# A decoder layer on one core: a residual whose bias row is added by a transfer, a shorter softmax, and another order of the first loads

## The chip, the cores and the metric

The kernel runs on one core of a Trainium2 chip. A core has a matrix engine (TensorE, PE in the profile, with its weight loads as PEld), a vector engine (VectorE, DVE), a scalar engine (ScalarE, ACT), a general engine (GpSimd, POOL) and SyncE (SP), and 16 DMA engines that move data between the large memory (HBM), the on-chip memory (SBUF) and within SBUF. Matrix products land in a separate small memory, PSUM, in banks of 512 floats a row. Every engine takes its instructions in order; they wait for one another by semaphores. The metric is the device time of one execution in microseconds (us), as the median of several.

## The reference

One decoder layer for 256 tokens of width 2048, all in float32:

1. `h = norm(alpha * x + 0.5 * swiglu(x))`, with a feed-forward block of inner width 5632. `norm` subtracts the mean of a token's row, divides by its standard deviation, multiplies by a gain row `g` and adds a bias row `b`.
2. A token mixer with two branches: attention with 16 heads (an indexer first picks 64 keys for every query, all others are masked; then a softmax over the scaled, masked scores and a weighted sum of the values), and a gated linear recurrence of width 2560. Both are gated, merged and multiplied by an output matrix: `h = norm(alpha * h + merged @ w_out)`.
3. `h = norm(alpha * h + 0.5 * swiglu(h))` with a second feed-forward block.

So there are three norms and three residual additions. Steps 2 and 3 need `alpha * h`, that is `alpha * (normalized * g + b)`, as the start of their sum.

## The kernel before, in words

**Products.** Every product is done in pairs of rounded numbers: a float32 weight piece `raw` is split into `wh` (rounded, ScalarE, line 243) and `wl` (the rest, VectorE, line 244), and activations likewise. Three matmuls, high by high, high by low, low by high, make one product (lines 694, 695, 697). In part of the products a scheme with seven in place of eight block products is used; for it VectorE makes sums of weight blocks (lines 206, 210, 213) and of activations (`left`, lines 592 to 598). The weights arrive as pieces of 128 x 1024 floats (`raw`, 512 KB) or of twice that (`rf`). Class `Weights` holds the list of all pieces in the order of use: `load_to` issues their transfers on SP, up to ten pieces ahead of use, into 5 `raw` buffers and 3 `rf` buffers; `split_to` issues the two splits, 4 pieces ahead, into 5 buffers; `unit` hands out the operands.

**Background steps.** Whenever `unit` takes up a new piece, it calls `bg.step()`, which advances every background generator by one `yield`. So a generator's `yield`s place its instructions in the program, one step per weight piece. The residuals, the heads' softmax and small tables are such generators.

**Order.** For PE, SP and POOL the order of the instructions is the order of the program text. For VectorE and ScalarE a planner sets the order from costs that it assumes; `issue_after(ins)` queues an instruction behind another one of the same engine. Whatever order comes out is then fixed: an engine whose next instruction has to wait holds up all that is behind it.

**Start.** Ten matmuls on a constant warm up PE (`warm_up`, line 439). The input `x`, transposed, is loaded in 8 chunks of 256 KB (`load_x_fm`, line 444), and each is split in two halves (`split_x`, lines 451 and 452). SP issues chunk 0, the first weight piece in two halves, chunk 1 and the second piece. The chunks 2 to 7 and the pieces 2 and 3 follow only when a one-column copy on VectorE (line 571), which writes into chunk 2's buffer, has waited for the first split. POOL issues the transfers of `cols` (224 columns of gains, biases and other per-channel values, line 459) and of `posi` (the positions, line 461) at once. `consts`, which makes sine and cosine tables from them, is a background generator.

**Residual.** `residual` prepares `alpha * (y * g + b)` in the tiles `Y[t][nb]`: two halves `t` of 128 tokens and four column blocks `nb` of 512. For each block POOL loads the rows of `g` and `b`, copied over all 128 partitions (`row`, line 649, 256 KB each), and in the first residual also two tiles of `Y` that had been put away in HBM (line 658). In the next steps VectorE does, for each `t`, `y = y * ALPHA * gr` (line 662) and `y = br * ALPHA + y` (line 664). With its `yield`s a block takes five steps. It runs twice: beside the merge of the two branches and the first part of the output product (1385 to 1466 us), and at the start of the second feed-forward block (1559 to 1622 us). The tiles `gr`, `br`, `Y` and many others share 53 buffers.

**Partial sums by transfer.** In the feed-forward blocks, halves of the output product are copied from PSUM with a factor (line 1109) and added to `Y` by a transfer of POOL with `accum_op=OP.add` (line 1110). These 80 transfers are the only adding ones.

**Heads.** `head` computes the scores of one head for two query blocks, 128 and 256 keys wide, into one PSUM tile of 384 columns. VectorE then scales them and adds the mask `bias`, which is 0 or -1e30 (line 1279), finds the negated maximum of each part (line 1284, two instructions), ScalarE takes the exponential with its sum (line 1287), VectorE divides (lines 1289, 1291), PE transposes (line 1295), ScalarE copies (line 1298) and PE multiplies by the values (lines 1301, 1302). Four heads are in work at a time, beside the products of the gates; at the end `bg.drain` runs what is left.

**End.** `OuterNorm.finish` normalizes the last tile of 128 tokens in four blocks. `first` (line 948) subtracts the mean and multiplies by `g`, `second` (line 952) multiplies by the inverse deviation and adds `b`, both on VectorE; for two of the blocks PE does the second part with a diagonal matrix (`by_pe`, line 967) and ScalarE copies the result (line 968). `leave` (line 956) issues the output transfers on SP.

Of the kernel before, what the change touches and what calls it, by code (L numbers as in the profile page):

```python
# [11 lines left out]
AF = mybir.ActivationFunctionType  # L12
OP = mybir.AluOpType
AX = mybir.AxisListType.X

P = 128
# [3 lines left out]
NK = D // P  # L20
# [9 lines left out]
ALPHA = 2.0 ** 0.25  # L30
THETA = 500000.0
TOPK = 64
NEG = -1e30
TAKEN = -3e38
ATT_SCALE = 128.0 ** -0.5
# [96 lines left out]
class Weights:  # L132
# [85 lines left out]
    def split_to(self, i, step=PIECE):  # L218
        nc = self.nc
        while self.split <= min(i, len(self.pieces) - 1):  # L220
            form = self.pieces[self.split][1]
            self.load_to(self.split)
            k = self.key(self.split)
            if self.split in self.wides:
                h, l = ([self.wide() for _ in range(2)] for _ in range(2))
                for c in range(2):
                    src = self.raw[k][:, c * 512:(c + 1) * 512]
                    nc.scalar.activation(h[c], src, AF.Copy)
                    nc.vector.tensor_tensor(l[c], src, h[c], op=OP.subtract)
                self.hl[self.split] = (h, l)  # L230
                del self.raw[k]
                self.split += 1
                continue
            h, l = (self.pool.tile([P, PIECE], F32R, name=f"w{s}{self.split}", tag=f"w{s}", bufs=HL_BUFS)
                    for s in "hl")
            n = self.size(self.split)
            if form:
                parts = [(self.operand(k, form), *(x[:, :n].rearrange("p (f r c) -> p f r c", r=4, c=P)
                                                   for x in (h, l)))]
            else:  # L240
                parts = [tuple(x[:, q:min(n, q + step)] for x in (self.raw[k], h, l)) for q in range(0, n, step)]
            for src, hp, lp in parts:
                nc.scalar.activation(hp, src, AF.Copy)  # L243
                self.last = nc.vector.tensor_tensor(lp, src, hp, op=OP.subtract)  # L244
            self.hl[self.split] = (h, l)
            if form in (None, FORMS[-1]):
                del self.raw[k]
            self.split += 1
# [71 lines left out]
def tile_layer(ctx, tc, x_fm, x_tm, pos, f1a, f1o, wA, wki, wB, wG, lru, wab, wrb, wo, f2a, f2o,  # L320
               cols_d, ln1_g, ln1_b, ln2_g, ln2_b, ln3_g, ln3_b, out):
    nc = tc.nc
# [4 lines left out]
    V, A, T, G = nc.vector, nc.scalar, nc.tensor, nc.gpsimd  # L327
# [96 lines left out]
    W = Weights(nc, pool, pieces, bg.step)  # L424
# [5 lines left out]
    xraw = [U("x") for _ in range(NK // 2)]  # L430
# [12 lines left out]
    def load_x_fm(k2):  # L443
        nc.sync.dma_start(xraw[k2], x_fm[:, k2 * 512:(k2 + 1) * 512])

    def split_x(k2):
        r = []
        for c in range(2):
            src = xraw[k2][:, c * S:(c + 1) * S]
            hl = UHL("xs")  # L450
            A.activation(hl[:, 0], src, AF.Copy)
            V.tensor_tensor(hl[:, 1], src, hl[:, 0], op=OP.subtract)
            r.append(hl)
        return r

    xs = []
    W.load_to(1, load_x_fm)
    cols = C([P, NCOLS], "cols")
    G.dma_start(cols, cols_d)
    posi = C([P, 2], "posi", I32)  # L460
    G.dma_start(posi, pos)
    tri = C([P, P], "tri")
    jp = tri.bitcast(I32)
    G.iota(jp, pattern=[[1, P]], base=0, channel_multiplier=-1)
# [21 lines left out]
        yield  # L486

    def consts():
        V.tensor_scalar(tri, jp, 0.0, NEG, op0=OP.is_gt, op1=OP.mult)
        posf = SM(2)  # L490
        V.tensor_copy(posf, posi)
        yield
        ang = SM(32)
        for t in range(2):
            V.tensor_scalar(ang[:, t * 16:t * 16 + 16], invf, posf[:, t:t + 1], None, op0=OP.mult)
        yield
        for dst, turn, shift in ((sn, 0.0, 0.0), (cs, 0.25, 1.5707963267948966)):
            k = SM(32)
            r = SM(32)
            V.tensor_scalar(k, ang, 0.15915494309189535, turn, op0=OP.mult, op1=OP.add)  # L500
            V.tensor_scalar(k, k, 12582912.0, None, op0=OP.add)
            V.tensor_scalar(k, k, 12582912.0, None, op0=OP.subtract)
            V.scalar_tensor_tensor(r, k, -6.28125, ang, op0=OP.mult, op1=OP.add)
            V.scalar_tensor_tensor(r, k, -0.0019350051879882812, r, op0=OP.mult, op1=OP.add)
            yield
            V.scalar_tensor_tensor(r, k, -3.019916050195849e-07, r, op0=OP.mult, op1=OP.add)
            V.tensor_scalar(r, r, shift, None, op0=OP.add)
            V.tensor_scalar(r, r, 3.1415925, -3.1415925, op0=OP.min, op1=OP.max)
            A.activation(dst.rearrange("p a b -> p (a b)"), r, AF.Sin)
            yield  # L510
# [56 lines left out]
    with tc.manual_schedule():  # L567
        for k2 in range(4):
            xs += split_x(k2)
            if k2 == 0:  # L570
                V.tensor_copy(xraw[2][:, :1], xs[0][:, 1, :1])
                W.load_to(3, load_x_fm)
                for j in range(4, NK // 2):
                    load_x_fm(j)
            W.split_to(k2, (256, 512, PIECE, PIECE)[k2])
        for k2 in range(4, NK // 2):
            xs += split_x(k2)

    def later(gen, ins):
        while True:  # L580
# [71 lines left out]
    def residual(g, b, away=None):  # L652
        for nb in range(4):
            gr, br = row(g, nb, "gr"), row(b, nb, "br")
            if away:
                for t in range(2):
                    Y[t][nb] = U("y")
                    G.dma_start(Y[t][nb], away[t][nb])
            yield
            for t in range(2):  # L660
                y = Y[t][nb]
                V.scalar_tensor_tensor(y, y, ALPHA, gr, op0=OP.mult, op1=OP.mult)
                yield
                V.scalar_tensor_tensor(y, br, ALPHA, y, op0=OP.mult, op1=OP.add)  # L664
                yield


# [249 lines left out]
    class OuterNorm(Norm):  # L917
# [18 lines left out]
        def finish(self):  # L936


            with tc.high_priority():
                self.chain(1)  # L940
            sums = {}
            for nb, o, w in ((0, 0, 512), (1, 0, S), (1, S, S)):
                ps = sums[nb, o] = BP()[:, :w]
                T.matmul(ps, ident, self.rows[1][nb][:, o:o + w], start=True, stop=False)

            def first(t, nb):
                y = Y[t][nb]
                V.scalar_tensor_tensor(y, y, self.mv[t], self.rows[0][nb], op0=OP.subtract, op1=OP.mult)

            def second(t, nb, o=0, w=512):  # L950
                y = Y[t][nb][:, o:o + w]
                V.scalar_tensor_tensor(y, y, self.r[t], self.rows[1][nb][:, o:o + w], op0=OP.mult, op1=OP.add)
                leave(t, nb, o, w)

            def leave(t, nb, o=0, w=512):
                nc.sync.dma_start(out[t * P:(t + 1) * P, nb * 512 + o:nb * 512 + o + w], Y[t][nb][:, o:o + w])

            for nb in range(4):
                first(0, nb)
            for nb in range(4):  # L960
                second(0, nb)
            diag = U("dg")[:, :P]
            A.activation(diag, ident, AF.Copy, scale=self.r[1])

            def by_pe(nb, o=0, w=512):
                ps, y = sums[nb, o], Y[1][nb][:, o:o + w]
                T.matmul(ps, diag, y, start=False, stop=True)
                A.activation(y, ps, AF.Copy)

            first(1, 2)  # L970
            first(1, 0)
            by_pe(0)
            second(1, 2)
            leave(1, 0)
            first(1, 1)
            by_pe(1, 0, S)
            by_pe(1, S, S)
            first(1, 3)
            second(1, 3, 0, S)
            second(1, 3, S, S)  # L980
            leave(1, 1)
# [159 lines left out]
    bias = C([P, 3 * P], "bias")  # L1141
# [126 lines left out]
    def head(h):  # L1268
# [5 lines left out]
        ps = BP()  # L1274
# [1 line left out]
        T.matmul(ps[:, P:3 * P], q[:, P:], k, start=True, stop=True)  # L1276
        yield
        s = U("s")[:, :3 * P]
        V.scalar_tensor_tensor(s, ps[:, :3 * P], ATT_SCALE, bias, op0=OP.mult, op1=OP.add)
        nm = SM(2)  # L1280
        sm = SM(2)
        part = (s[:, :P], s[:, P:])
        for t in range(2):
            V.tensor_reduce(nm[:, t:t + 1], part[t], axis=AX, op=OP.max, negate=True)
        yield
        for t in range(2):
            A.activation(part[t], part[t], AF.Exp, bias=nm[:, t:t + 1], accum_out=sm[:, t:t + 1])
        yield
        V.reciprocal(sm, sm)
        for t in range(2):  # L1290
# [2 lines left out]
        ps = BP()  # L1293
# [6 lines left out]
        ps = BP()  # L1300
# [61 lines left out]
    for nb in range(4):  # L1362
        g, got = got, fetch(ga[nb + 1]) if nb < 3 else None
        s, _ = product(ya, ya_forms, YA_FAST[nb])
# [71 lines left out]
    for j in range(NR + LAG):  # L1436
        if j < NR:
            s = block3(hs)
# [5 lines left out]
            for tap in (2, 1, 0):  # L1444
                sh = 3 - tap
                V.scalar_tensor_tensor(xc[:, sh:], raw[:, :S - sh], col("conv_w", tap * NR + j), xc[:, sh:],
                                       op0=OP.mult, op1=OP.add)
# [5 lines left out]
        if j >= LAG:  # L1453
# [6 lines left out]
            ps = banks[c - 1]  # L1460
            for n in range(2):
                mm3(ps[:, n * S:(n + 1) * S], xcs[i], W.unit(P), False, n == 1)
            vw, t = U("vw"), T1()
# [164 lines left out]
```

## Time and profile before

| | us |
|---|---|
| median of 3 runs | 2239.33 |
| lowest and highest | 2238.25, 2239.59 |
| the profiled execution, its own time | 2239.67 |
| its span in the profile | 2237.9 |
| PE busy in the span | 2223.3 |
| VectorE busy | 2106.7 |
| ScalarE busy | 1429.8 |
| POOL busy | 125.0 |

The profiled execution took 2239.67 us; 1.8 us of that lie outside its span. A row of a list of waits names an engine and a line, what it waited for, and the total, the number and the longest of these waits. A row of the timeline gives the start, the duration, the engine, the line, the operation, the tile written and the tiles read with their shapes, the number of instructions in the row, and in brackets the idle time ahead of it with what ended it. A row of a table by windows gives for each engine the busy time in that stretch and the number of its instructions, then the granted TensorE clock, the share of time in which the 16 DMA engines were busy, and GB/s. In a list by queue, q1 carries SP's transfers and q0 POOL's, with packets, megabytes and the share of the time of 16 engines. The ends of matmuls are modelled, so a gap of PE in these rows is somewhat shorter than the real one.

### The profile page before, as it was taken

What the parts mean: (1) busy time and instruction counts of PE and PEld (TensorE: products, weight loads), DVE (VectorE), ACT (ScalarE), POOL (GpSimd) and SP (SyncE); (2) the same over time, 40 slices, a digit from 0 to 9 for tenths busy, and PEclk for the clock granted to TensorE, in tenths of its full rate; (3) what the DMA queues carried; (4) which work ended last, traced back from release to release, by engine and by line L of the source; (5) the groups of instructions that cost most, each with busy time, mean ns of one, the idle gap of its engine ahead of it and who ended that gap; (6) DMA issues with size and microseconds to landing.
All of it is one profiled execution on the core that took longest, in us unless ns stands there. A gap on an engine that the chain in (4) does not pass through costs nothing. (4 is left out here: it accounts for less than half of the span.)

```text
span 2237.9 us, 38642 instructions
## 1 busy us (share of the span) xinstructions
PE 2223.3 (99%) x14582; PEld 2056.6 (92%) x14582; DVE 2106.7 (94%) x3037; ACT 1429.8 (64%) x1995; POOL 125.0 (6%) x195
## 2 busy tenths in 40 slices
PE   9999999999999999999999999999999999999998
PEld 7999999999998898899999999998889999999997
DVE  8999999999999999899868879999999999999997
ACT  7666666666656655665567786555666666666663
POOL 0000000000001000001000002100000000000001
PEclk9999999999999999999999999999999999999999
DMA  9776666666675555648666668766677667676655
GB/s 328 240 227 232 233 214 226 236 222 236 225 241 194 187 198 177 210 132 302 199 192 194 197 189 324 266 214 205 229 228 230 237 220 239 223 243 215 219 200 188
DMA packets 126186, 498.61 MB, mean 223 GB/s; under 512 B 14608, under 2 KB 17424, under 8 KB 107312
## 3 DMA queue, kind: packets, MB, share of 16 engines
q1 hardware_dynamic: 107424, 451.98, 57.9%
q0 software_dynamic: 18576, 44.17, 8.4%
q8 instruction: 114, 1.87, 0.3%
q14 instruction: 72, 0.59, 0.1%
HBM read 464.63 MB, written 10.49 MB: 212 GB/s over the span
## 5 line engine op out<-in xcount | busy, mean ns | idle before, releaser
L243 ACT ACTIVATE wh<-raw 128x1024 fp32r<-128x1024 f32 (+1 forms) x569 | 575.0, 1028 | 288.6 <-PE mm L695 164.4
L244 DVE TENSOR_TENSOR wl<-raw,wh 128x1024 fp32r<-128x1024 f32 (+1 forms) x569 | 661.9, 1183 | 79.8 <-ACT wh L243 78.6
L243 ACT ACTIVATE wh<-rf 128x1024 fp32r<-128x1024 f32 (+1 forms) x438 | 393.5, 915 | 191.6 <-PE mm L695 103.6
L244 DVE TENSOR_TENSOR wl<-rf,wh 128x1024 fp32r<-128x1024 f32 (+1 forms) x438 | 450.9, 1042 | 7.2 <-ACT wh L243 1.5
L694 PE MATMUL mm<-wh,hs 128*128 128x512 f32 (+1 forms) x872 | 297.3, 350 | 0.0
L695 PE MATMUL mm<-wh,hs 128*128 128x512 f32 (+1 forms) x872 | 292.1, 344 | 0.0
L694 PE MATMUL mm<-wh,g 128*128 128x512 f32 x656 | 249.5, 380 | 1.9 <-DVE z L1076 1.9
L695 PE MATMUL mm<-wh,g 128*128 128x512 f32 x656 | 248.8, 379 | 0.5 <-DVE g L810 0.5
L243 ACT ACTIVATE wh<-ws 128x1024 fp32r<-128x1024 f32 x146 | 155.2, 1063 | 123.9 <-PE mm L695 71.7
L694 PE MATMUL bp<-wh,sh 128*128 128x256 f32 x876 | 213.6, 278 | 0.0
L695 PE MATMUL bp<-wh,sl 128*128 128x256 f32 x876 | 210.7, 275 | 0.0
L697 PE MATMUL mm<-wl,hs 128*128 128x512 f32 (+1 forms) x872 | 205.0, 344 | 0.0
L206 DVE TENSOR_TENSOR ws<-rf 128x1024 f32<-128x1024 f32 x146 | 178.3, 1221 | 8.8 <-DMA rf<-wab 2.8
L244 DVE TENSOR_TENSOR wl<-ws,wh 128x1024 fp32r<-128x1024 f32 x146 | 178.1, 1220 | 2.8 <-ACT wh L243 2.6
L694 PEld LDWEIGHTS mm<-wh,hs 128*128 128x128 f32 x872 | 165.8, 190 | 15.3 <-issue 1.3
L695 PEld LDWEIGHTS mm<-wh,hs 128*128 128x128 f32 x872 | 165.9, 190 | 13.6
L1404 PE MATMUL mm<-hs,wh 128*128 128x256 f32 x640 | 176.4, 276 | 0.0
L1405 PE MATMUL mm<-hs,wh 128*128 128x256 f32 x640 | 176.0, 275 | 0.0
L1406 PE MATMUL mm<-hs,wl 128*128 128x256 f32 x640 | 176.0, 275 | 0.0
L695 PEld LDWEIGHTS bp<-wh,sl 128*128 128x128 f32 x876 | 168.1, 192 | 1.2
L694 PEld LDWEIGHTS bp<-wh,sh 128*128 128x128 f32 x876 | 168.0, 192 | 1.2
L697 PE MATMUL mm<-wl,g 128*128 128x512 f32 x656 | 168.3, 379 | 0.0
(374 smaller groups left out, 4886.5 us busy)
## 6 DMA issues: line engine op xcount, KB each, us to landing
rf<-f1a SPq DMA_DIRECT2D x57, 1024.0 KB, 6.2
rf<-f2a SPq DMA_DIRECT2D x57, 1024.0 KB, 6.0
raw<-f1o SPq DMA_DIRECT2D x88, 512.0 KB, 7.8
raw<-f2o SPq DMA_DIRECT2D x88, 512.0 KB, 7.8
raw<-wB SPq DMA_DIRECT2D x80, 512.0 KB, 4.5
raw<-f2a SPq DMA_DIRECT2D x62, 512.0 KB, 3.9
raw<-f1a SPq DMA_DIRECT2D x61, 512.0 KB, 3.9
raw<-wG SPq DMA_DIRECT2D x54, 512.0 KB, 4.2
```

Of the source, the lines that this page charges most:

```text
L206: v.tensor_tensor(t, b[:, 0:4:3], b[:, 1:2].to_broadcast([P, 2, 4, P]), op=OP.add)
L243: nc.scalar.activation(hp, src, AF.Copy)
L244: self.last = nc.vector.tensor_tensor(lp, src, hp, op=OP.subtract)
L694: T.matmul(ps, xh, w[0], start=start, stop=False)
L695: T.matmul(ps, xl, w[0], start=False, stop=False)
L697: T.matmul(ps, xh, w[1], start=False, stop=stop)
L1404: T.matmul(ps, w[0], xh, start=first, stop=False)
L1405: T.matmul(ps, w[0], xl, start=False, stop=False)
L1406: T.matmul(ps, w[1], xh, start=False, stop=last)
```

## The change

The change has five parts.

1. **First loads.** SP issues the chunks 0 to 3 of `x` and the pieces 0 to 3 in turn, and then chunks 4 to 7, with no wait. The one-column copy of line 571 goes.
2. **Column table.** `cols` and `posi` are no longer issued first. A one-column copy on VectorE writes into `cols` behind the last split of `x`, and POOL's two transfers wait for it. `consts` starts eight steps later.
3. **Residual.** ScalarE scales the bias row once a block (`br = ALPHA * br`, queued behind the newest `wh`), VectorE does only `y = y * ALPHA * gr`, and POOL adds `br` to `y` by a transfer, SBUF to SBUF, one for each `t`. Rows and the first product are two steps apart in place of one, and a block takes four steps in place of five. The adding transfers stand in POOL's queue ahead of the next block's rows.
4. **Heads.** One instruction a part reads the scores from PSUM, adds the mask, multiplies by `-ATT_SCALE` and finds the minimum; it replaces the scaling over both parts and the maximum of each. The exponential takes its input with a factor of -1.
5. **End.** `first(1, 0)` stands ahead of `first(1, 2)`.

```diff
@@ Weights.split_to
-                nc.scalar.activation(hp, src, AF.Copy)
+                self.last_h = nc.scalar.activation(hp, src, AF.Copy)
                 self.last = nc.vector.tensor_tensor(lp, src, hp, op=OP.subtract)
@@ tile_layer, start
-    W.load_to(1, load_x_fm)
+    W.load_to(3, load_x_fm)
+    for k2 in range(4, NK // 2):
+        load_x_fm(k2)
     cols = C([P, NCOLS], "cols")
-    G.dma_start(cols, cols_d)
     posi = C([P, 2], "posi", I32)
-    G.dma_start(posi, pos)
@@ consts
+        for _ in range(8):
+            yield
         V.tensor_scalar(tri, jp, 0.0, NEG, op0=OP.is_gt, op1=OP.mult)
@@ tile_layer, the first splits
             xs += split_x(k2)
-            if k2 == 0:
-                V.tensor_copy(xraw[2][:, :1], xs[0][:, 1, :1])
-                W.load_to(3, load_x_fm)
-                for j in range(4, NK // 2):
-                    load_x_fm(j)
             W.split_to(k2, (256, 512, PIECE, PIECE)[k2])
         for k2 in range(4, NK // 2):
             xs += split_x(k2)
+        V.tensor_copy(cols[:, :1], xs[-1][:, 1, :1])
+    G.dma_start(cols, cols_d)
+    G.dma_start(posi, pos)
@@ residual
             yield
+            yield
+            with tc.issue_after(W.last_h.ins):
+                A.activation(br, br, AF.Copy, scale=ALPHA)
             for t in range(2):
                 y = Y[t][nb]
                 V.scalar_tensor_tensor(y, y, ALPHA, gr, op0=OP.mult, op1=OP.mult)
-                yield
-                V.scalar_tensor_tensor(y, br, ALPHA, y, op0=OP.mult, op1=OP.add)
+                G.dma_start(y, br, accum_op=OP.add)
                 yield
@@ OuterNorm.finish
+            first(1, 0)
             first(1, 2)
-            first(1, 0)
             by_pe(0)
@@ head
-        V.scalar_tensor_tensor(s, ps[:, :3 * P], ATT_SCALE, bias, op0=OP.mult, op1=OP.add)
         nm = SM(2)
         sm = SM(2)
         part = (s[:, :P], s[:, P:])
         for t in range(2):
-            V.tensor_reduce(nm[:, t:t + 1], part[t], axis=AX, op=OP.max, negate=True)
+            a, b = t * P, (1 + 2 * t) * P
+            V.tensor_tensor_reduce(s[:, a:b], ps[:, a:b], bias[:, a:b], -ATT_SCALE, -2 * NEG, OP.add, OP.min,
+                                   nm[:, t:t + 1])
         yield
         for t in range(2):
-            A.activation(part[t], part[t], AF.Exp, bias=nm[:, t:t + 1], accum_out=sm[:, t:t + 1])
+            A.activation(part[t], part[t], AF.Exp, scale=-1.0, bias=nm[:, t:t + 1], accum_out=sm[:, t:t + 1])
```

## The prediction

> **What bounds the kernel now.** I read the page first, for the engine that sets the end, then the list of what PE waited for, then the timeline around each of those waits.
>
> ```profile
> span 2237.9 us, 38642 instructions
> PE 2223.3 (99%) x14582; PEld 2056.6 (92%) x14582; DVE 2106.7 (94%) x3037; ACT 1429.8 (64%) x1995; POOL 125.0 (6%) x195
> PEclk9999999999999999999999999999999999999999
> ```
> PE is busy 99% of the span at its full clock, and the change leaves its matmuls alone. So the change can gain only what PE now waits, and lose what it makes PE wait.
>
> ```profile
> PE mm L694 <- ACT wh L243: 2.4, 3, 1.4
> PE mm L694 <- DVE z L1076: 1.9, 1, 1.9
> PE bp L967 <- DVE y L948: 1.2, 1, 1.2
> PE bp L1295 <- ACT pT L1298: 0.7, 1, 0.7
> PE mm L695 <- DVE g L810: 0.5, 1, 0.5
> ```
> These five rows are the places that the change touches: three waits at the start (2.4 us), two beside the second residual (1.9 + 0.5), one where the heads end (0.7) and one in the last norm (1.2). Without the last they come to 5.5 us, 0.25% of the span: the most that can be won. VectorE at 94% is the engine that can take it back.
>
> **The start, loads and column table.** The first and the last of the three in the timeline:
>
> ```profile
> 8.55 1.15 ACT L243 ACTIVATE wh<-raw 128x512 fp32r<-128x512 f32 x2 [0.53 <-DMA raw<-f1a]
> ...
> 18.21 1.06 ACT L243 ACTIVATE wh<-raw 128x1024 fp32r<-128x1024 f32 x1 [0.35 <-DMA raw<-f1a]
> ```
> Each time ScalarE begins as a weight piece lands, and PE a microsecond later. So the landings set PE's pace until the third, at 18.2 us; PE gains what this third landing moves. SP's issues do not set the landings: the DMA engines never run out of SP's work. The table by windows and the list of queues from 3 to 7 us, where `cols` and `posi` pass:
>
> ```profile
> 5.00:6.00 1.00, 1.00 (x5) 0.79 (x4) 1.00 (x4) 0.77 (x4) 0.00 (x0) 1.00 0.82 238
> 6.00:7.00 1.00, 1.00 (x7) 0.86 (x6) 0.79 (x3) 0.39 (x2) 0.00 (x0) 1.00 1.00 402
> q1 hardware_dynamic: 528, 1.15, 78.9%
> q0 software_dynamic: 80, 0.12, 11.3%
> ```
> In these 4 us POOL's two transfers take 11.3%, 0.45 us of each of the 16 engines, and 9.8% (0.39 us) stays empty although SP's chunk 1 and piece 1 are queued; the dip to 238 GB/s falls where the small `posi` lands. Moved behind the last split, the two free 0.45 us for certain and up to 0.84 us if the empty time was theirs. I take 0.8, since the rate is back at 402 GB/s as soon as they are gone. Loads in a row are worth nothing alone, but they are needed: with the old wait, the earlier landing would meet a queue without work. Bounds: 0, if one of the 16 engines is late for another reason and the landing waits for that one; 2.4, if a queue filled without a break lands all three pieces in time. The moved transfers later take the same 0.45 us at about 20 us, behind the last of the three waits; if that cover is gone, a fourth wait of this size appears. The copy of 128 x 1 that goes and the one that comes are equal. `consts` comes eight steps later; its tables are first read behind the whole first feed-forward block.
>
> **The second residual.** VectorE is what PE waits for here.
>
> ```profile
> 1590.90 1.23 DVE L206 TENSOR_TENSOR ws<-rf 128x1024 f32<-128x1024 f32 x1 [1.86 <-DMA rf<-f2a]
> 1637.31 0.45 PE L694 MATMUL mm<-wh,g 128*128 128x512 f32 x1 [1.87 <-DVE z L1076]
> 1590.00:1637.00 47.00, 44.91 (x266) 40.37 (x264) 46.10 (x65) 27.00 (x37) 1.80 (x2) 1.00 0.70 232
> 1590.90:1618.00 27.10, 3.45 (x5) 1.00 0.59 215
> 1618.00:1637.00 19.00, 0.69 (x1) 1.00 0.85 255
> ```
> From 1590.9 us, when a late `rf` lands, VectorE works without a pause (46.1 of 47 us) until PE has to wait for its sum. The last two rows are line 664 alone: six of its eight adds, 3.45 + 0.69 = 4.1 us, lie in this stretch, and five of them ahead of the smaller wait near 1618.4. They all go. 4.1 is more than the 2.4 us of both waits, so as far as VectorE's work goes both close. The scaling on ScalarE (27 of 47 us busy) is one instruction in place of two adds, four a residual; its nearest row, a copy of the same shape, is below. What takes back:
>
> ```profile
> 1559.36 0.58 POOL L649 DMA_DIRECT2D gr<-ln_g  x1 [0.27 <-issue]
> 1576.24 0.69 DVE L662 SCALAR_TENSOR_TENSOR y<-y,gr 128x512 f32<-128x512 f32 x1
> 1600.28 1.29 DVE L662 SCALAR_TENSOR_TENSOR y<-y,gr 128x512 f32<-128x512 f32 x2
> 1614.91 0.69 DVE L662 SCALAR_TENSOR_TENSOR y<-y,gr 128x512 f32<-128x512 f32 x1
> DMA to landing us min/median/max: 3.7/5.9/12.3
> L1110 POOL DMA_DIRECT2D y<-yd x80: 852/945/1240, 72.3 to 2182.9; - x80
> L1109 ACT ACTIVATE yd<-mm x80: 573/582/591, 71.4 to 2181.8; 128x512 f32<-128x512 f32 x80
> q0 software_dynamic: 288, 0.52, 43.0%
> 1580.00:1590.00 10.00, 10.00 (x48) 8.76 (x47) 9.05 (x17) 6.37 (x10) 1.08 (x2) 1.00 0.91 288
> ```
> (a) *DMA time.* The q0 row is a stretch of 7 us (1626 to 1633) with two of today's adding transfers: 43% of 7 us is 3.0, so one costs the 16 engines 1.5 us. The first block's two come at about 1580 to 1590 us, where the engines are 91% busy and bring that late `rf`. It can land up to 3.0 us later; I take 1.5, since its queue and POOL's share the time. [...]
> (b) *Rows behind sums.* Today POOL issues rows from 1559 us, ahead of use: the first product is at 1576. The row without a line's name is the landing of line 649's transfers. With the change every next block's rows stand in POOL's queue behind the adding transfers, which wait for this block's products. From the last product to the landed row: 0.95 (the adding transfer's issue) + 0.58 (the row's issue) + 5.9 = 7.4 us. The next block's first product is three steps on. In the busy stretch VectorE passes 10 steps in some 15 us (the products of the second block at 1600.3, those of the fourth from 1614.9), 1.5 a step, 4.4 us for three. So it can stand still 3.0 us for each of the last two blocks, 6 in all; behind the waiting product then stand the `wl` that PE needs. Below nothing is excluded, as less work cannot make the rows earlier. But the planner knows that rows take time and may put the product after more `wl`; no product of today stands idle for its inputs. I take 1.0 in all, near that end.
>
> Net: 4.1 - 1.5 - 1.0 = 1.6 us of the 2.4 come back. Bounds: 2.4, and 4.1 - 3.0 - 6.0 = -4.9.
>
> **The first residual.**
>
> ```profile
> L662 DVE SCALAR_TENSOR_TENSOR y<-y,gr x16: 686/690/698, 1429.2 to 1618.8; 128x512 f32<-128x512 f32 x16
> 1385.47 0.54 POOL L649 DMA_DIRECT2D gr<-ln_g  x1
> 1435.24 0.54 POOL L1348 DMA_DIRECT2D gf<-gd  x1 [0.47 <-PE bp L1503]
> 1476.82 1.29 DVE L1517 SCALAR_TENSOR_TENSOR gf<-gf,stg 128x512 f32<-128x512 f32 x2
> 1473.61 1.06 ACT L243 ACTIVATE wh<-raw 128x1024 fp32r<-128x1024 f32 x1 [1.53 <-PE mm L695]
> ```
> Here POOL runs 44 us ahead (rows at 1385, the first product at 1429). That lead goes: the fetch of the last gates (line 1348), now issued until 1435, moves behind three blocks' adding transfers. Three rounds of 7.4 us from 1431 are 1453, with four fetches of 0.54 some 1456, landed about 1465 (the rows' 5.9 to twice that); VectorE needs them at 1476.8. It still fits with 10 us. ScalarE waits for PE here, so the splits are ahead and a short stop of VectorE is covered. Cost 0; without that cover it is the price under (b).
>
> **Heads.**
>
> ```profile
> L1284 DVE TENSOR_REDUCE s<-s 128x1 f32<-128x128 f32 (+1 forms) x32 | 9.7, 347 | 0.1
> L1279 DVE SCALAR_TENSOR_TENSOR s<-bp,bias 128x384 f32<-128x384 f32 x16 | 8.6, 551 | 0.0
> L1306 DVE TENSOR_TENSOR ya<-bp,ya 128x256 fp32r<-128x256 f32 x13 | 5.3, 418 | 0.0
> L1287 ACT ACTIVATION_READ_ACCUMULATOR s<-s,s 128x1 f32 x32 | 6.1, 189 | 0.0
> ```
> A head costs 0.55 + 2 x 0.35 = 1.25 us now. The new instruction is not in the trace. Nearest: line 1306, 256 columns with one input in PSUM, 0.42; for 128 columns I take 0.3, between half of it and all of it. That is 0.7 a head, 0.5 saved, 8 us of VectorE over 16 heads. If each also shows a read-out like ScalarE's 0.19, it is 1.1 and 0.15 saved. Either way PE's products of the gates hide it, except in the drain, where PE waits 0.7 us for a copy behind these chains: I take 0.4 there, bounds 0 and 0.7. [...]
>
> **The last norm.**
>
> ```profile
> 2230.10 0.73 DVE L948 SCALAR_TENSOR_TENSOR y<-y,s,row 128x512 f32<-128x512 f32 x1
> 2230.98 2.36 PE L967 MATMUL bp<-y,dg 128*128 128x512 f32 x6 [1.24 <-DVE y L948]
> 2232.86 0.88 DVE L952 SCALAR_TENSOR_TENSOR y<-y,s,row 128x256 f32<-128x256 f32 x2
> ```
> PE's wait here is for the block that now comes first, so it shrinks by some 0.3 us. But VectorE does the same eight instructions without a gap to 2233.74, and the last output transfers wait for these. Gain 0.
>
> **Sum.** 0.8 + 1.6 + 0 + 0.4 + 0 = 2.8 us. The profiled execution took 2239.67, 0.34 above the median of 2239.33: 2236.87, or 2236.5 against the median. About 0.2% (4.5 us) is what a measurement of this kernel can tell from no change.
>
> **Rivals.** Times are against the median, like the forecast.
> - *All waits close.* A queue that is never short lands the three first pieces in time, and VectorE's 4.1 us suffice: 5.5 us, 2233.8. For it: the waits are few and each is one that a part addresses. Against: the DMA engines are full at the start. Chance 0.25.
> - *The wait moves.* At the second residual VectorE waits for rows what it saves in adds, as in (b) with 1.5 for `rf` and 2.6 for rows. Only the start's 0.8 stays: 2238.5. Chance 0.20.
> - *Slower.* (b) and (a) at their full price: VectorE stands still at 1590 to 1620 us in POOL's order of sums and rows: 3.0 + 6.0, and 6.4 more where one row lands as late as the latest did (12.3 in place of 5.9), 15.4 in all. Less the 4.1 saved PE is 11.3 later, with the start's 0.8 back 2249.8. It costs from 4.1 us of waiting on, and passes the 0.2% from 9.4. For it: VectorE has no pause there. Against: today no product waits for its inputs. Chance 0.12.
> - *The table frees nothing.* The first loads land as now, since one slow DMA engine holds each landing; 2.0 us remain, 2237.3. Chance 0.08.
>
> The forecast has 0.35. **Range** 2232.8 to 2241.5: it holds the first, second and last rival and the slower one's beginning; what is left out is most of that one and times under the first. Faster by over 0.2% (below 2234.9) is the first rival and 0.05 of the forecast, 0.30; slower 0.11; within 0.59.
>
> **What would show it.** Right: the first piece after chunk 1 lands some 0.8 us earlier and the three waits shrink to about 1.6; line 664 is gone, POOL has 16 more adding transfers, and PE's wait for line 1076 is below 1 us. Wrong: VectorE idle ahead of line 662, ended by a row's transfer; a wait of line 206 for `rf` longer than 4 us; a PE wait for `wl` in a place that had none; the heads' new instruction longer than 0.5 us on average.

## The result and the profile after

The changed kernel takes 2257.75 us (median; 2256.11 to 2258.86), the kernel before, measured beside it, 2239.03 (2238.25 to 2239.59). The ratio is 1.0083, with a 95% interval of 1.0066 to 1.0101: 18.7 us slower, where 2236.5 was forecast and the range ended at 2241.5. The profiled execution of the changed kernel took 2258.86 us, 1.86 outside its span. In its code line 649 issues a row, 658 the fetch of an earlier result, 662 is ScalarE's scaling of the bias row, 665 the product and 666 the adding transfer; `wh` and `wl` are still split in lines 243 and 244.

From the page of the changed kernel, the span, the engines' busy time and the granted clock in 40 slices:

```profile
span 2257.0 us, 38666 instructions
PE 2229.9 (99%) x14582; PEld 2060.5 (91%) x14582; DVE 2093.0 (93%) x3037; ACT 1432.8 (63%) x2003; POOL 140.0 (6%) x211
PEclk9999999999999999999999999999999999999999
```

Seen from here little has happened: VectorE has 13.7 us less to do, and PE issues the same 14582 matmuls. The list of what PE waited for (us in total, times, longest) says where the time is:

```profile
PE mm L699 <- DVE wl L244: 9.0, 4, 6.0
PE mm L696 <- ACT wh L243: 5.9, 4, 3.8
PE bp L699 <- DVE wl L244: 1.4, 2, 0.7
```

These 16.3 us are waits for splits, 1.5 of them at the start. Before, PE waited for splits 2.4 us at the start and a few tenths elsewhere. The same list for VectorE and, in a second fence, for ScalarE:

```profile
DVE y L665 <- DMA y<-ys: 16.8, 3, 8.1
DVE y L665 <- DMA gr<-ln_g: 8.2, 3, 6.6
```
```profile
ACT br L662 <- DMA br<-ln_b: 41.7, 6, 10.6
```

So VectorE stands still 25.0 us ahead of line 665, in all six blocks that are not the first of their residual, and ScalarE 41.7 us ahead of line 662. The splits that PE needs are queued behind these instructions: ScalarE's next `wh` begins at 1455.27 us, behind a scaling that had waited 6.19 us, and VectorE's next `wl` at 1456.42, behind a product that had waited 3.83. What they wait for is in POOL's timeline at the first residual, from the last sum of block 0 to the first row of block 2 (start us, duration us, engine, line, instruction, in brackets the idle time before it and what ended it):

```profile
1429.85 0.87 POOL L666 DMA_DIRECT2D y<-br  x1 [0.58 <-DVE y L665]
1430.40 0.89 POOL L649 DMA_DIRECT2D gr<-ln_g  x1
1430.96 0.89 POOL L649 DMA_DIRECT2D br<-ln_b  x1
1431.50 1.41 POOL L658 DMA_DIRECT2D y<-ys  x2
1444.90 1.84 POOL L666 DMA_DIRECT2D y<-br  x2 [11.99 <-ACT wh L243]
1446.01 1.31 POOL L649 DMA_DIRECT2D gr<-ln_g  x1
```

The rows and fetches of block 1 are issued right behind the second sum of block 0, and those of block 2 not before the sums of block 1. Before the change POOL had issued the first block's rows 44 us ahead of their product (1385.47 and 1429.17), and the last block's fetches still 15 us ahead (1445.08 and 1460.35). The DMA list for 1430 to 1445 us has their landing (KB each, median us from issue to landing):

```profile
y<-ys POOLq DMA_DIRECT2D x2, 256.0 KB, 12.2
gr<-ln_g POOLq DMA_DIRECT2D x1, 256.0 KB, 9.1
br<-ln_b POOLq DMA_DIRECT2D x1, 256.0 KB, 11.1
```

VectorE's products, and its stops, in the first residual and (the last three rows) in the second:

```profile
1428.85 0.69 DVE L665 SCALAR_TENSOR_TENSOR y<-y,gr 128x512 f32<-128x512 f32 x1
1443.65 1.39 DVE L665 SCALAR_TENSOR_TENSOR y<-y,gr 128x512 f32<-128x512 f32 x2 [8.10 <-DMA y<-ys]
1455.48 0.69 DVE L665 SCALAR_TENSOR_TENSOR y<-y,gr 128x512 f32<-128x512 f32 x1 [3.83 <-DMA y<-ys]
1471.24 0.69 DVE L665 SCALAR_TENSOR_TENSOR y<-y,gr 128x512 f32<-128x512 f32 x1 [4.86 <-DMA y<-ys]
...
1605.73 1.29 DVE L665 SCALAR_TENSOR_TENSOR y<-y,gr 128x512 f32<-128x512 f32 x2 [0.73 <-DMA gr<-ln_g]
1616.65 1.29 DVE L665 SCALAR_TENSOR_TENSOR y<-y,gr 128x512 f32<-128x512 f32 x2 [0.83 <-DMA gr<-ln_g]
1630.78 0.69 DVE L665 SCALAR_TENSOR_TENSOR y<-y,gr 128x512 f32<-128x512 f32 x1 [6.62 <-DMA gr<-ln_g]
```

And PE's pauses in the same stretches, with the one of ScalarE's scalings that ends just before the second:

```profile
1444.01 0.48 PE L696 MATMUL mm<-wh,yr 128*128 128x512 f32 x1 [0.68 <-ACT wh L243]
...
1454.73 0.63 ACT L662 ACTIVATE br<-br 128x512 f32<-128x512 f32 x1 [6.19 <-DMA br<-ln_b]
1456.36 0.79 PE L696 MATMUL mm<-wh,yr 128*128 128x512 f32 x1 [3.76 <-ACT wh L243]
1465.30 1.13 PE L699 MATMUL mm<-wl,yr 128*128 128x512 f32 x4 [2.08 <-DVE wl L244]
...
1632.66 0.79 PE L699 MATMUL mm<-wl,hs 128*128 128x256 f32 x2 [5.99 <-DVE wl L244]
```

The first stop, of 8.10 us, costs PE 0.68 at once and 1.27 in two short waits for `wl` behind it (1446.57 and 1449.30 us): there are split pieces in hand, as the prediction said. The next ones find none, as VectorE is busy for 7.98 of the 7.99 us from the first stop to the second and has no time to split ahead again: where it stops 3.83 us and ScalarE 6.19, PE stops 3.76, and at the second residual VectorE's 6.62 become 5.99 of PE's.

The pauses cost twice. The table by windows, before and after, over the first residual (us; busy time and count of PE, PEld, DVE, ACT, POOL; granted clock; DMA share; GB/s):

```profile
1440.00:1475.00 35.00, 35.00 (x194) 31.47 (x193) 34.93 (x53) 18.98 (x24) 1.40 (x3) 1.00 0.65 208
```
```profile
1456.24:1459.65 3.41, 3.29 (x8) 2.63 (x9) 3.41 (x7) 3.41 (x6) 1.99 (x3) 0.50 0.45 92
1466.48:1469.89 3.41, 3.41 (x9) 2.65 (x8) 0.00 (x0) 0.00 (x0) 0.00 (x0) 0.50 0.92 262
1630.32:1637.15 6.83, 4.49 (x13) 3.76 (x14) 6.37 (x8) 5.21 (x7) 1.76 (x2) 0.50 0.50 94
1440.00:1475.00 35.00, 26.56 (x124) 21.64 (x123) 22.66 (x36) 14.50 (x21) 11.90 (x18) 0.90 0.80 233
```

The first fence is the kernel before, the second the changed one. Where PE ran 194 matmuls in 35 us it now runs 124, a lag of about 70/194 of 35 us, 12.6 us. Part of the loss is not waiting: in three stretches, two here and one at the second residual, the granted clock is 0.50. They last 13.65 us together, and PE is busy in 11.19 of them; the rest lies inside its pauses, above all the start of the third. In them a matmul of 512 columns begins 0.43 us after the one before it (1457.38 and 1457.81), at full clock 0.22 (1440.57 and 1440.79). So half of 11.19, some 5.6 us, is what they cost, by this estimate. With the 11.8 us by which all PE's listed waits have grown (21.6 from 9.8) it makes 17.4 of the 18.7 us. The page agrees: the span has grown by 19.1 us, PE's busy time by 6.6 for the same matmuls, and its idle time by 12.5. The clock row of the page does not show it, as its slices are 56 us long.

### The profile page after: what moved, and what is told of

It reads as the page before. It is cut to its first block, busy times and chain, and to the rows that moved or that the text cites. A ratio compares the mean times of both kernels' runs of the same rounds, so it can differ in the third digit from the quotient of the medians.

```text
span 2257.0 us, 38666 instructions
## 1 busy us (share of the span) xinstructions
PE 2229.9 (99%) x14582; PEld 2060.5 (91%) x14582; DVE 2093.0 (93%) x3037; ACT 1432.8 (63%) x2003; POOL 140.0 (6%) x211
## 5 line engine op out<-in xcount | busy, mean ns | idle before, releaser
L699 PEld LDWEIGHTS mm<-wl,hs 128*128 128x128 f32 x872 | 154.2, 190 | 21.7 <-DVE wl L244 6.2
```

What stands on the lines that cost most here:

```text
L699: T.matmul(ps, xh, w[1], start=False, stop=stop)
```

## The experiments

All times are medians; a ratio is to the kernel before, run beside it. Differences in us are differences of ratios times 2239. The explanation under test is that POOL's order makes the loss: rows and fetches stand behind sums that wait for products. Each expectation names its own theories by letters.

### The residual alone, and everything else alone

The changed kernel with the residual of before:

```
-            with tc.issue_after(W.last_h.ins):
-                A.activation(br, br, AF.Copy, scale=ALPHA)
...
-                G.dma_start(y, br, accum_op=OP.add)
+                yield
+                V.scalar_tensor_tensor(y, br, ALPHA, y, op0=OP.mult, op1=OP.add)
```

> The changed kernel with the residual of before put back (both VectorE operations, rows ahead in POOL's queue, no adding transfer); loads, column table, heads and last norm stay changed. Theory A (the loss comes from the residual alone, whose rows stand in POOL's queue behind the adding transfers): 2237 to 2239, the forecast's 0.8 us for the start and up to 0.7 for the heads' drain are all that is left, and TensorE's clock is whole. Theory B (another part shifts the planner's order of VectorE and that costs too): above 2242, with waits of PE beside the residual or the heads.

The kernel before with the changed residual, its start, heads and end as they were:

> The kernel before with the residual's part alone. Theory A: 2257 to 2260, as slow as the whole change or slower by what the start and the heads win; VectorE idle ahead of line 662's products, ended by rows or tiles of Y, some 24 us in all. Theory B: well below 2257, since the other parts would have their share in the loss.

Measured: without the changed residual 2237.90, ratio 0.9997 (0.9987 to 1.0007); with nothing but it 2260.26, ratio 1.0098 (1.0083 to 1.0113). The loss is the residual's, and the rest of the change loses nothing. The list of VectorE's waits in the second kernel has the two rows of the changed one again:

```profile
DVE y L665 <- DMA y<-ys: 17.5, 3, 8.4
DVE y L665 <- DMA gr<-ln_g: 7.9, 2, 6.9
```

### The order without adding transfers, and adding transfers with another order

POOL's place in the order can be had without any adding transfer: VectorE adds as before, ScalarE's scaling goes, and where the sum stood POOL copies one column of the finished block.

```
-            with tc.issue_after(W.last_h.ins):
-                A.activation(br, br, AF.Copy, scale=ALPHA)
...
                 V.scalar_tensor_tensor(y, y, ALPHA, gr, op0=OP.mult, op1=OP.mult)
-                G.dma_start(y, br, accum_op=OP.add)
+                V.scalar_tensor_tensor(y, br, ALPHA, y, op0=OP.mult, op1=OP.add)
+                G.tensor_copy(SM(1), y[:, :1])
```

> The changed kernel without adding transfers: VectorE does product and sum as before, and a one-column copy on POOL that reads the finished y stands where the adding transfer stood, so the next block's rows wait in POOL's queue for the sums in the same way. Theory A: the loss is there without any adding transfer, 2250 to 2262, somewhat less than in the changed kernel because the rows land sooner (5.9 us in the median in place of 8.6). Theory C: 2238 to 2241, as nothing is added by transfers.

The other way round, the sums are kept and the rows of the next block are issued one block earlier:

```
+        nxt = rows(0)
         for nb in range(4):
-            gr, br = row(g, nb, "gr"), row(b, nb, "br")
+            gr, br = nxt
...
             yield
+            nxt = rows(nb + 1) if nb < 3 else None
```

> The changed kernel, but each block's rows (and tiles of Y) are issued one block earlier, ahead of the former block's adding transfers in POOL's queue; the adding transfers, the scaling on ScalarE and the products stay. Theory A (order in POOL's queue): most of the loss goes, 2236 to 2243; VectorE's idle time ahead of the products falls from 24 us to under 6. Theory C (the adding transfers' own time on the 16 DMA engines, 16 x 1.5 us, crowds out weight pieces): stays above 2250.

Measured: the order alone 2261.99, ratio 1.0104 (1.0089 to 1.0119), as slow as the change; the sums with a lead of one block 2242.08, ratio 1.0012 (1.0002 to 1.0021). So what an adding transfer costs by itself is not the cause. The first was expected to be somewhat faster than the change, since its rows land sooner. They do (median 5.7 us), but POOL now waits for VectorE's adds too and issues the rows of block 1 at 1436.92 in place of 1430.40. In the second the list of VectorE's stops ahead of products is down to one row of the timeline, again a fetch, a little over the 6 us that were expected, and PE waits for a split 12.8 us later:

```profile
1443.45 0.69 DVE L671 SCALAR_TENSOR_TENSOR y<-y,gr 128x512 f32<-128x512 f32 x1 [6.30 <-DMA y<-ys]
...
1459.41 1.13 PE L705 MATMUL mm<-wl,yr 128*128 128x512 f32 x4 [3.18 <-DVE wl L244]
```

If this row is the rest of the loss, a longer lead removes it. All rows and fetches first, then the products and sums of all four blocks:

```
+        got = []
         for nb in range(4):
-            gr, br = row(g, nb, "gr"), row(b, nb, "br")
+            got.append((row(g, nb, "gr"), row(b, nb, "br")))
...
+        for nb in range(4):
+            gr, br = got[nb]
+            got[nb] = None
             yield
```

> The changed kernel, but each residual issues the rows and earlier results of all four blocks first and its products and adding transfers after them, so that nothing that a product reads stands behind a sum in POOL's queue. With a lead of one block the time was 2242.1, with one stop of 6.3 us ahead of a product left, ended by an earlier result's transfer, and PE's wait of 3.2 us for wl. Theory A (the lead decides): the stop and that wait go, VectorE never waits for DMA ahead of a product, 2236 to 2239, level with the kernel that keeps the old residual (2237.9). Theory C (the adding transfers' own DMA time costs the rest): 2241 to 2243, with no stop ahead of a product but later weight pieces (waits of line 206 for rf over 4 us in all). Theory B (sixteen more tiles held at once starve the ring that all stages share): over 2243, with PE or VectorE waits in other lines.

Measured: 2235.80 (2234.97 to 2237.47), ratio 0.9985 (0.9976 to 0.9994). Theory A holds, with a time 0.2 us under its interval: this version is faster than both kernels, by 3.4 us against the one before. The group of its products has no idle time before it:

```profile
L669 DVE SCALAR_TENSOR_TENSOR y<-y,gr 128x512 f32<-128x512 f32 x16 | 10.6, 685 | 0.0
```

### Which residual

All rows first in one residual, the change's order in the other:

```
-            bg.add("main", residual(ln1_g, ln1_b, away))
+            bg.add("main", residual_ahead(ln1_g, ln1_b, away))
```

(this one leaves the second residual late; the same edit at `ln2_g, ln2_b` leaves the first late).

> The changed kernel with its order of rows behind sums in the first residual alone; in the second, all rows first. All rows first in both gave 2235.8, the change 2257.8. Theory A (as the trace of the change reads: most of the loss, 13 of 19 us of PE, is at the first residual, where VectorE stops 16.8 us for earlier results and PE then runs at half its clock for some 7 us): 2246 to 2252, with these stops and none ahead of the second residual's products. Theory P (as predicted: at the first residual the splits are ahead, a stop of VectorE is covered, and the price falls at the second): 2235 to 2239.

> The other half: all rows first in the first residual, the change's rows behind sums in the second alone. Theory A (the trace of the change: stops of 8.2 us ahead of three products, PE's wait of some 6 us for wl and 6.8 us at half clock after it, less what PE gains by waiting nowhere else): 2240 to 2245. Theory P (the whole loss has its place here, as the prediction's slower rival had it): 2249 or more. Theory N (the two halves are not additive, the second stops only because the first shifted it): 2235 to 2239.

Measured: late at the first residual only, 2249.02, ratio 1.0044 (1.0030 to 1.0059); late at the second only, 2245.78, ratio 1.0026 (1.0016 to 1.0035), 0.8 us above theory A's interval, though its ratio comes to 2244.8. Against all rows first these are 13.2 and 9.2 us, by the ratios; together they give 22.4, and the change against all rows first is 21.9. The two halves add up, and neither is needed for the other. The second half is one stop and what follows it, in this kernel's list of PE's waits and, in the second fence, its table by windows:

```profile
PE mm L721 <- DVE wl L244: 6.4, 2, 5.9
```
```profile
1615.37:1622.20 6.83, 5.30 (x14) 4.19 (x15) 6.17 (x9) 5.21 (x7) 1.78 (x2) 0.50 0.52 104
```

5.9 us of waiting and half of the 5.30 us in which PE was busy at half clock are 8.6 of the 9.2; the stretch begins inside the pause, so the rest of its 6.83 us is in the 5.9 already.

### What in a round is late, and whom it holds

The earlier results are fetched first, only the rows stay behind the sums:

```
+        if away:
+            for nb in range(4):
+                for t in range(2):
+                    Y[t][nb] = U("y")
+                    G.dma_start(Y[t][nb], away[t][nb])
         for nb in range(4):
             gr, br = row(g, nb, "gr"), row(b, nb, "br")
-            if away:
...
```

> The changed kernel, but the first residual fetches the earlier results of all four blocks first; its rows, and those of the second residual, stay behind the sums as in the change. Theory A (the two fetches at the end of each round, which the prediction's chain left out, make the round long: 14.8 us in place of 7.4): VectorE's stops at the first residual fall from 16.8 us to below 6, the time from 2257.8 to 2244 to 2250. Theory B (the rows themselves land as late, 9 to 11 us after their issue, since the queues are full): the stops stay above 12 us, now ended by a row, and the time at 2253 to 2258.

Measured: 2254.45, ratio 1.0064 (1.0049 to 1.0079). The time is theory B's; VectorE's stops at the first residual are 10.8 us, between the two. From its timeline:

```profile
1442.54 1.29 DVE L666 SCALAR_TENSOR_TENSOR y<-y,gr 128x512 f32<-128x512 f32 x2 [4.99 <-DMA gr<-ln_g]
1451.22 0.69 DVE L666 SCALAR_TENSOR_TENSOR y<-y,gr 128x512 f32<-128x512 f32 x1 [2.85 <-DMA gr<-ln_g]
1465.13 0.69 DVE L666 SCALAR_TENSOR_TENSOR y<-y,gr 128x512 f32<-128x512 f32 x1 [2.95 <-DMA gr<-ln_g]
```

The fetches make 6 us of the 16.8, and 3.3 us of the time by the medians (4.3 by the ratios, whose intervals overlap); the rest of the stop is there with the rows alone.

ScalarE stands longer than VectorE, and its splits are queued behind the scaling. Without the scaling (the bias row is then added unscaled):

```
-            with tc.issue_after(W.last_h.ins):
-                A.activation(br, br, AF.Copy, scale=ALPHA)
```

> The changed kernel without ScalarE's scaling of the bias row (the row is added unscaled, so this part of the computation is left out). In the change ScalarE stands 41.7 us in six waits for that row, with weight splits queued behind, and VectorE 25.0 us in six waits ahead of its products. Theory V (VectorE's stops alone are enough, since the gain row and the earlier results land as late): VectorE's stops stay at 20 to 25 us, PE's waits are for wl, 2252 to 2259. Theory S (ScalarE's stop ahead of the splits is what PE feels): the time falls to 2240 to 2248, though VectorE still stops.

Measured: 2259.51, ratio 1.0092 (1.0074 to 1.0110). Half a microsecond above theory V's interval, and far from theory S: VectorE's stops, 27.1 us where 20 to 25 were expected, are enough. PE's wait for `wh` moves to `wl`:

```profile
PE mm L697 <- DVE wl L244: 14.8, 6, 7.6
PE bp L697 <- DVE wl L244: 3.0, 3, 2.0
```

### The other terms by themselves

The start, heads and end of the change, the first residual as before, the second with sums and all rows first; the kernel before with the changed start alone; and with the changed heads alone:

```
-            bg.add("main", residual(ln1_g, ln1_b, away))
+            bg.add("main", residual_old(ln1_g, ln1_b, away))
```

> The start, heads and end of the change; the first residual as before, with VectorE's adds; the second with adding transfers, all rows first. So it measures the term of the second residual without POOL's order of rows and sums. The kernel with the old residual everywhere has 2237.9 and PE waits 1.4 us for line 1076's sum and 0.3 for a split there. Theory A (4.1 us of adds less are enough when rows are there in time): these two waits are below 0.3 us together, 2235.5 to 2237.5. Theory C (the adding transfers delay rf by 1.5 to 3.0 us and eat most of it): the wait of VectorE for rf grows by that, PE's stays at 1 us or more, 2237.5 to 2239.5.

> The kernel before, with the start of the change alone: first loads in a row, column table and positions fetched behind the last split, constants eight steps later. Theory A (the table's and positions' time in the queues goes back to the loads): PE's waits for the first splits shrink from 2.4 us by 0.8 to 1.6, 2237.5 to 2238.6, and the third piece's split starts 0.8 to 1.1 us earlier than 18.21. Theory B (one slow DMA engine holds each landing, the table frees nothing): the split starts at 18.0 or later, waits 2.0 us or more, 2239.0 to 2239.6.

> The kernel before, with the head softmax of the change alone. Theory A (VectorE's part of a head is 0.7 us and two read-outs of 0.08 in place of 1.25, some 0.4 saved; only the drain shows it): PE's wait of 0.7 us at the end of the heads falls below 0.2, 2238.3 to 2238.9. Theory B (the softmax's shorter step shows nowhere, since another copy is late in the drain): the drain's wait stays or moves to another line with 0.5 us or more, 2239.0 to 2239.5.

Measured: 2236.82, ratio 0.9988 (0.9979 to 0.9997); 2238.31, ratio 0.9995 (0.9986 to 1.0004); 2238.67, ratio 0.9997 (0.9987 to 1.0006). In the first PE's wait for line 1076's sum is gone from the list; the 0.8 us for a split that the list has are at the start (18.11 us). The other two intervals hold "no change" as well as what was expected, and the rows must decide. For the start two of them cannot: the third piece's split begins at 17.65 us with the changed start, and at 17.70 in the kernel that has only the heads changed, so this time moves by half a microsecond from one execution to the next. All fourteen traces together point one way. The three kernels with the start of before have 18.21, 17.70 and 17.53 us, the eleven with the changed one 16.57 to 17.65, median 17.00; PE's waits for these first splits are 1.3 to 2.4 us in the three and 0.2 to 2.0, median 1.0, in the eleven. The values overlap a little, and it is three kernels against eleven. For the heads, PE's wait of 0.7 us in the drain is gone, here and wherever the heads are changed, while it is 0.7 in the two other kernels that keep the old heads. The new instruction shows (group rows by form: busy us, mean ns):

```profile
L1284 DVE CUSTOM_DVE_ANT_0 s<-bp,bias 128x256 f32<-128x256 f32 x16 | 6.7, 420 | 0.0
L1284 DVE CUSTOM_DVE_ANT_0 s<-bp,bias 128x128 f32<-128x128 f32 x16 | 4.5, 283 | 0.0
L1284 DVE DVE_READ_ACCUMULATOR2_ANT s<- 128x1 f32 x32 | 2.7, 83 | 0.0
```

## Why the prediction was wrong

- **The first residual, "Cost 0": this step failed.** It was worth 13.2 us. Three things in it did not hold. A round was put at 7.4 us, with the median landing of 5.9 taken from rows with none of the residual's sums between them (from 1430 to 1445 us POOL's queue took 22.6% of the 16 engines' time in the kernel before and 37.6% in the changed one), and without the two fetches that stand at the end of each round. From the last product of a block to the first of the next, the timeline shows 1429.5 to 1443.65: 14.1 us, with landings of 9 to 12. Then the deadline that was tested was that of the last gates at 1476.8 us, and the three rounds of products themselves were not set against VectorE's own pace; a VectorE that is busy 34.93 of 35 us has no room for a stop of 8, 4 and 5 us. And "a short stop of VectorE is covered" is right for the first one alone (8.10 us, of which PE saw 0.68 at once and 1.27 after it): the cover is a stock of split pieces, and the row that showed ScalarE ahead said nothing of how fast the stock is filled again.
- **Rows behind sums, (b): right mechanism, wrong size.** The first two of the three stops at the second residual are 0.73 and 0.83 us, the last 6.62, 8.2 in all, where 1.0 was taken and 6.0 was the bound. That no product of the kernel before stood idle was taken as a sign that the planner would place products late enough; with rows issued far ahead it could not have been otherwise, so it was no evidence. With the half clock that followed, this order cost 9.2 us.
- **The slower rival had the cause** (rows behind sums, VectorE still, splits behind it) and a chance of 0.12. It put the whole loss at 1590 to 1620 us. The larger part came at the first residual, which it left at nothing, and the second half stopped at 1624 to 1631.
- **ScalarE's scaling** was counted as work only, not as a wait. It stood 41.7 us for the bias row. The kernel without it is as slow, so this adds nothing to the loss here, but the step was missing.
- **The DMA time of the sums, (a): not seen.** Over the whole span VectorE's wait for `rf` from `f2a` was 2.5 us before and 1.6 after; with all rows first it is 2.6, while PE still no longer waits for VectorE's sum. At the place that the step named, the late `rf` at the second residual, it is 0.4 to 1.9 us in the four kernels with the old residual there, and at most 1.8 in those with adding transfers, among them the changed one with none.
- **The second residual's 4.1 us of adds** were enough, once the rows were there: with sums there alone PE waits for line 1076 no more, and the kernel is 2.0 us under the one with the old residual in both by the ratios, 1.1 by the medians (each ratio with an interval of some 2 us to either side). The step forecast 1.6 and allowed at most 2.4.
- **The start, 0.8: borne out in the rows, but only by all traces together.** In the changed kernel the third split began 1.03 us earlier (17.18 us) and the two waits left were 1.5 us, but a kernel with the start of before also shows 1.5. Over all traces the third split comes 0.7 us earlier and the waits are 0.5 shorter, by the medians. From 3 to 7 us SP's transfers take 96.9% of the DMA engines in the changed kernel, in place of 78.9%, so most of the empty time went too. The time of the start alone, -1.1 us by the ratio (-3.1 to +0.9), agrees with 0.8 and with 0.
- **The heads: the instruction was sized right.** 0.42 + 0.28 is the 0.70 forecast, with two read-outs of 0.08 it is 0.87 a head. The drain's wait went, all of its 0.7 us where 0.4 was taken. The trace has a read-out of its own behind each of the 32, of 83 ns, where the prediction's other case took 0.19 us.
- **The last norm, 0: held.** PE's wait there is 0.9 us in place of 1.2, and 2.0 in the kernel with all rows first, the fastest of them all; no time hangs on it.

With the order mended, all terms but (b) are left, and the kernel is 3.4 us faster (1.3 to 5.4); the sum for the whole change had been 2.8, which is 3.8 without (b). What the prediction lacked was the one thing that its own list of signs named first, VectorE idle ahead of the product, ended by a transfer.

## What to carry to other kernels

When a transfer that waits for a computed result is put into a queue that also fetches, ask first what stands behind it in that queue: each later fetch now starts when the result is there (here the rows of block 2 at 1446.01 us, behind the sums of block 1 at 1444.90), and its landing is to be taken from rows with the queue as full as it will be (8.6 us in the median here, where 5.9 was taken), with every transfer of the round counted. Do not count a stock of work ahead twice: here it covered the first stop (8.10 us cost PE 1.95) and not the next (3.83 on VectorE and 6.19 on ScalarE cost 3.76), as the engine that fills it had no spare time in between. Where such an operation saves work, issue all that the later rounds read ahead of the first of them; that order made the same edit a gain here (2235.80 us in place of 2257.75).

## What the runs showed of the hardware that was not expected

At three of the changed kernel's four pauses of PE of 2 us or more the granted clock falls to 0.50, for 3.41 or 6.83 us: from 1456.24 us at the end of the pause of 3.76, from 1466.48 behind the one of 2.08, and from 1630.32 within the one of 5.99. With one residual late, 6.83 us are at 0.50 too, from 1454.91 with the first and from 1615.37 with the second. In the changed kernel three tenths of the loss are this (some 5.6 of 18.7 us, by the estimate above). The length of the pause alone does not decide: the pause of 2.08 us at 1465.30 is followed by such a stretch, the one of 2.00 is not, as the timeline and the window behind it show,

```profile
1566.91 1.07 PE L864 MATMUL bp<-ident,y 128*128 128x128 f32 x8 [2.00 <-DVE y L883]
```
```profile
1567.00:1577.00 10.00, 10.00 (x57) 8.77 (x58) 9.53 (x29) 7.61 (x27) 1.81 (x3) 1.00 0.44 121
```

and the pause of 3.18 in the kernel with a lead of one block is not either, whose window reads:

```profile
1450.00:1470.00 20.00, 16.82 (x90) 14.62 (x90) 19.27 (x31) 7.86 (x11) 3.16 (x5) 1.00 0.94 265
```

What else decides is not shown by these runs.

The landing of a transfer of 256 KB from POOL's queue went from 3.7/5.9/12.3 us (minimum, median, maximum over the rows of line 649) to these in the changed kernel:

```profile
DMA to landing us min/median/max: 3.9/8.6/13.2
```

With the same order and no sums it is 3.8/5.7/12.8, and with sums and all rows first 4.2/5.8/12.9. So in these kernels the landing is longer where sums stand between the rows, 8.6 us in place of 5.7 to 5.9. That alone is not the loss: the kernel with 5.7 is as slow as the change, and with a lead of one block the median is 10.4 us and the time 2242.08.
